# A two-layer encoder step on one core: the query norm behind its projection, zero products at the beginning, joined last outputs, and the final norm in two halves

## The chip, the cores and the metric

The kernel runs on one core of one Trainium2 chip. The metric is device time in microseconds (us), from launch to the end of the program. Three runs of the kernel before gave 2819.73 to 2820.59 us, median 2820.01 us.

## The reference

One step of a hybrid encoder trunk is computed for two request groups that share the weights: 512 new frames and 64 frames of a running stream, 576 tokens together, model width 1024, two layers. Cut to what matters here:

```
x = x + 0.5 * (silu(norm(x) @ w_gate) * (norm(x) @ w_up)) @ w_down        # ffn1, width 2816
h = norm(x); proj = h @ w_in                                              # token mixer
q = rmsnorm(c_q, q_norm) @ w_uq                                           # c_q: 256 columns of proj
y_a = latent attention (8 heads, chunk mask) of q against c_kv            # MLA
y_b = RWKV-7 recurrence (8 heads, 64x64 state), written by chunks of 64
x = x + concat(y_a, y_b) @ w_out
x = x + cross attention(norm(x), 256 memory tokens)
x = x + 0.5 * swiglu(norm(x))                                             # ffn2
y = rmsnorm(x, final_norm)                                                # after both layers
```

All of it is in float32. Every norm is an RMS norm: rsqrt of the mean square over the features, times a gain. The scale of one token is one number, so a norm can be applied before or after a linear projection.

## The kernel before

The activations lie with the features on the 128 partitions and the 576 tokens along the row: x is 8 tiles of 128x576. Where a product needs one accumulator bank, the tokens are cut into two halves `hs` of 288 (HT). A float32 product is done as three products in a rounded format: both operands are split into a high and a low part (`split`, L244 to L249: ScalarE copies the high part, VectorE subtracts to get the low part), and `mm3` (L313 to L317) issues high x high, high x low and low x high into one accumulator. So every weight block of 128x512 costs one ScalarE copy (`whi` or `sh`) and one VectorE subtraction (`wlo` or `sl`) before TensorE can use it.

Feed-forward: the 22 blocks of the inner width go by pairs. The first two pairs (`PLAIN`) are plain products, gate then up (`plain_gate`, `plain_up`); the pairs from 2 to 10 use a scheme of seven products on sums and differences of blocks (`gate`, `up`, `sums`), the sums of the weights being made on VectorE as well (`add` in `factors`). After every second pair `all_outputs` multiplies the finished activations by the output weights `wds` and adds the result to x, one VectorE instruction for each 128x288 block (L521). The last pair, 10, has its outputs alone, with the weights `wd` of its own. The weights come in the order of the list `order`, through a ring of six split blocks (four `whi`/`wlo`, two `sh`/`sl`).

Norm (`Norm`, L360 to L390): ScalarE writes x times the gain as a high part `xnh` (L370), VectorE the low part `xnl` (L371); ScalarE squares (L376), VectorE adds them up in `nacc` (L378), a product with ones sums over the partitions (L386), and `rsqrt` (L300, L349, L350) gives `rstd`, which is applied to the result of the product. So the product starts before the norm is known.

Mixer: the columns of w_in are projected in a list of steps, among them `queries` (two tiles `lx` for c_q, their squares, and the sum of the squares on GpSimd, L851) and, after `rotated`, `normed`: the sum over partitions by a product with ones (L360), `rsqrt` (L300, L349, L350), then c_q times gain and scale (L867) and the split into `qnh`, `qnl`. Attention follows: the value factors `vph`, `vpl`, the keys `kfh`, `kfl` and `kch`, `kcl`, then for each pair of heads the queries `qf` and their split. The products that make them write banks `g`, of which there are two; `sm` is another pair of banks. The recurrence runs beside it: VectorE inverts triangular matrices (L781, L782, tiles `x` of 72 partitions), copies of the state are laid into `VS` (L1036, L1037), and products `pp` (L1052) start the chunks.

The order of the instructions on each engine is made by a scheduler when the program is built, from the order of the code and modelled durations; each engine then runs its list strictly in order, and waits at an instruction whose operand is not there.

The last feed-forward ends in the final norm (`final`, `tail`): squares of x by tile, sums of pairs on VectorE and GpSimd, six products with ones for each half (L1411), `rsqrt`, and the scaled output in six VectorE (L1415) and two GpSimd instructions for each half. The transfers to `y` go out by pairs of tiles.

## Time and profile before

| what | value |
|---|---|
| median of three runs | 2820.01 us |
| the profiled execution: its time | 2819.02 us |
| its span, first to last instruction | 2817.0 us |
| TensorE busy | 2733.7 us (97%) |
| VectorE busy | 2124.5 us (75%) |
| ScalarE busy | 1351.2 us (48%) |
| GpSimd busy | 100.1 us (4%) |
| mean granted TensorE clock | 0.991 |

Engines are PE (TensorE), DVE (VectorE), ACT (ScalarE), POOL (GpSimd) and SP (SyncE, which issues the transfers). The span leaves out 2 us of the execution's own time. A stretch in which TensorE is idle is read from the waits and from windows; what ended an idle stretch stands behind an arrow.

### The profile page before, as it was taken

The numbers are of one execution on the slowest core, as the hardware profiler recorded it, in microseconds if no ns is written. First come the engines' busy times: TensorE is split into PE (matmuls) and PEld (weight loads), VectorE is DVE, ScalarE is ACT, GpSimd is POOL, SyncE is SP. The second block draws the span as 40 slices with busy tenths as digits, with TensorE's granted clock in tenths as the row PEclk, the third lists the DMA queues.
The fourth block names the chain that finished last, engine by engine and source line by source line (L and its number), as shares of the span: only waits on it lengthen the run. The fifth ranks groups of instructions, "written<-read, shape, count | busy, mean of one in ns | idle before, by whom it ended". The sixth has DMA issues, their size and how long they took to land.

```text
span 2817.0 us, 55885 instructions
## 1 busy us (share of the span) xinstructions
PE 2733.7 (97%) x22284; PEld 2629.8 (93%) x22284; DVE 2124.5 (75%) x4356; ACT 1351.2 (48%) x2781; POOL 100.1 (4%) x197
## 2 busy tenths in 40 slices
PE   8999999979999999999999999998999999999998
PEld 8999999968889899999999999997888899999998
DVE  8888876875676678777788777769666765887776
ACT  5544446355544544444444444554555445444443
POOL 0000001010000000000000000012000000000000
PEclk9999999989999999999999999999999999999999
DMA  5333333652233222222223222346433332222221
GB/s 192 101 111 114 112 124 110 158 142 91 92 119 117 72 97 72 92 93 92 94 71 105 91 90 91 109 105 171 118 98 123 98 117 64 91 91 90 92 93 60
DMA packets 187573, 293.21 MB, mean 104 GB/s; under 512 B 87066, under 2 KB 113050, under 8 KB 187138
## 3 DMA queue, kind: packets, MB, share of 16 engines
q1 hardware_dynamic: 185010, 285.46, 32.3%
q0 software_dynamic: 2304, 4.20, 0.6%
q8 instruction: 175, 2.87, 0.4%
q14 instruction: 84, 0.69, 0.1%
HBM read 250.36 MB, written 41.63 MB: 104 GB/s over the span
## 4 chain that ended last, share of the span: by engine, by line
PE 92%; DVE 4%; ACT 2%; issue 1%; DMA 0%; DVEq 0%; SPq 0%; POOL 0%; ACTq 0%
PE b L315 18%; PE b L316 18%; PE b L317 18%; PE mm L315 4%; PE mm L316 4%; PE mm L317 4%; PE g L315 4%; PE g L316 3%; PE g L317 3%; PE sm L1028 2%; PE pp L1028 2%; PE sc L315 2%; PE pp L1052 1%; PE sc L316 1%; PE sc L317 1%; PE tp L981 1%
## 5 line engine op out<-in xcount | busy, mean ns | idle before, releaser
L247 ACT ACTIVATE whi<-wraw 128x512 fp32r<-128x512 f32 (+1 forms) x493 | 305.4, 623 | 543.5 <-PE b L316 264.9
L248 DVE TENSOR_TENSOR wlo<-wraw,whi 128x512 fp32r<-128x512 f32 (+1 forms) x493 | 333.8, 680 | 117.6 <-ACT whi L247 99.9
L317 PE MATMUL b<-s,wlo 128*128 128x288 f32 x1388 | 408.0, 295 | 0.0
L316 PE MATMUL b<-s,whi 128*128 128x288 f32 x1388 | 406.7, 294 | 0.0
L315 PE MATMUL b<-s,whi 128*128 128x288 f32 x1388 | 405.5, 296 | 0.0
L315 PE MATMUL b<-xnh,whi 128*128 128x288 f32 x1168 | 344.5, 298 | 11.5 <-ACT xnh L370 7.6
L316 PE MATMUL b<-xnl,whi 128*128 128x288 f32 x1168 | 346.2, 297 | 3.4 <-DVE xnl L248 1.8
L317 PE MATMUL b<-xnh,wlo 128*128 128x288 f32 x1168 | 343.6, 296 | 0.0
L521 DVE SCALAR_TENSOR_TENSOR x<-b,x 128x288 f32<-128x288 f32 x448 | 196.8, 455 | 132.0 <-PE b L317 131.7
L316 PEld LDWEIGHTS b<-s,whi 128*128 128x128 f32 x1388 | 261.2, 188 | 0.0
L317 PEld LDWEIGHTS b<-s,wlo 128*128 128x128 f32 x1388 | 261.2, 188 | 0.0
L315 PEld LDWEIGHTS b<-s,whi 128*128 128x128 f32 x1388 | 259.5, 188 | 0.0
L315 PEld LDWEIGHTS b<-xnh,whi 128*128 128x128 f32 x1168 | 219.5, 189 | 13.1 <-ACT xnh L370 7.6
L316 PEld LDWEIGHTS b<-xnl,whi 128*128 128x128 f32 x1168 | 220.3, 189 | 5.7 <-DVE xnl L371 2.9
L316 PE MATMUL b<-s,sh 128*128 128x288 f32 x756 | 224.1, 297 | 0.0
L317 PE MATMUL b<-s,sl 128*128 128x288 f32 x756 | 223.1, 296 | 0.0
L315 PE MATMUL b<-s,sh 128*128 128x288 f32 x756 | 223.0, 296 | 0.0
L317 PEld LDWEIGHTS b<-xnh,wlo 128*128 128x128 f32 x1168 | 220.3, 189 | 0.0
L315 PE MATMUL mm<-xnh,whi 128*128 128x288 f32 x688 | 204.2, 298 | 5.2 <-DVE shp L391 1.8
L316 PE MATMUL mm<-xnl,whi 128*128 128x288 f32 x688 | 205.1, 298 | 1.0 <-DVE xnl L371 0.9
L317 PE MATMUL mm<-xnh,wlo 128*128 128x288 f32 x688 | 204.1, 297 | 0.0
L247 ACT ACTIVATE whi<-S 128x512 fp32r<-128x512 f32 x171 | 107.9, 631 | 165.8 <-PE b L316 161.9
(474 smaller groups left out, 7241.4 us busy)
## 6 DMA issues: line engine op xcount, KB each, us to landing
wraw<-in_wgu SPq DMA_DIRECT2D x131, 512.0 KB
wraw<-in_wds SPq DMA_DIRECT2D x48, 512.0 KB
sraw<-in_wgu SPq DMA_DIRECT2D x45, 512.0 KB
wraw<-in_win SPq DMA_DIRECT2D x36, 512.0 KB
wraw<-in_wd SPq DMA_DIRECT2D x21, 512.0 KB
sraw<-in_wds SPq DMA_DIRECT2D x16, 512.0 KB
wraw<-in_wmk SPq DMA_DIRECT2D x16, 512.0 KB
wraw<-in_wmv SPq DMA_DIRECT2D x16, 512.0 KB
```

Source lines behind the costliest of these rows:

```text
L247: ACT.activation(out=h, in_=src, func=AF.Copy)
L248: by.tensor_tensor(out=lo, in0=src, in1=h.bitcast(F32), op=ALU.subtract)
L315: PE.matmul(out, wh, ah, start=first, stop=False, **kw)
L316: PE.matmul(out, wh, al, start=False, stop=False, **kw)
L317: return PE.matmul(out, wl, ah, start=False, stop=last, **kw)
L521: DVE.scalar_tensor_tensor(out=o, in0=p, scalar=0.5, in1=o, op0=ALU.mult, op1=ALU.add)
L981: PE.transpose(pT[0:n, c0:c0 + nq], pe_[e][0:nq, kt * 128:kt * 128 + n], ident[0:nq, 0:nq])
L1028: PE.matmul(o, *f(p4, e), start=(n == 0 and p4 == 0), stop=(n == len(terms) - 1), skip_group_check=True)
L1052: i = PE.matmul(p[:, p4], bk[half(e), p4], ck[half(e), p4, 0:128], start=True, stop=True)
```

## The change

1. Beginning. The transfer of x tile 0 goes ahead of the first weight block and the early constants follow tile 2. If the first weights are given (layer 0, ffn1), 22 products of a zero tile are issued ahead of everything. In every feed-forward the first half (`parts=(0,)`, 24 products) of the first `up` is issued right behind the first gate, ahead of the product with ones of the norm.

2. End of each feed-forward. Pairs 8, 9 and 10 have their outputs together (`last_outputs`): 18 products in one accumulator instead of 12 and 6, and one VectorE addition to x instead of two. The outputs of 8 and 9 no longer stand between the gate and the up of pair 10. The weights come in the new order. In the last feed-forward of the kernel the second group of four tiles is done by halves, and the final norm of half 0 is issued behind the second of the four outputs of half 1.

3. Queries. c_q times gain is split right behind its projection, without the scale of the norm; the sum of the squares moves from GpSimd to VectorE; the scale goes into its own tile `rq` and is multiplied onto `qf` (128x576, once for each of the 8 heads). In the first pair of heads the products take banks `g` and `sm` by turns. The state is loaded into `VS` by two transfers instead of two copies.

4. Final norm. Each half has its own squares, six VectorE additions in a chain, two products with ones instead of six, and the outputs on VectorE and ScalarE alone.

The list of instructions has 14 more on TensorE (22 zero products, less 8 products with ones), 39 fewer on VectorE and 6 more on ScalarE.

```diff
         for k in range(8):
-            if k in (0, 3):
+            if k in (1, 4):
                 given.append(Weights(I["wgu1"][0, 0, len(given)]))
             t = st([128, T], "x")
             SP.dma_start(t, I["x"][k])
             x.append(t)
+            if k == 2:
+                SP.dma_start(cst[:, 0:early], I["cst"][:, 0:early])
...
+        if given:
+
+            z, pz = st([128, 2, HT], "s", F32R), ps1("b")[:, 0:HT]
+            POOL.memset(z[:, 0].bitcast(F32), 0.0)
+            for _ in range(22):
+                PE.matmul(pz, z[:, 0, 0:128], z[:, 0], start=True, stop=True)
...
-            if (p - PLAIN) % 2:
+            if (p - PLAIN) % 2 and p < NF // 2 - 2:
                 order += [[wds[l, (p - PLAIN) // 2, m]] for m in range(4)]
-        order += [[wd[l, PLAIN, g]] for g in range(2)]
+        for g in range(2):
+            order += [[wd[l, PLAIN, g]]] + [[wds[l, (NF // 2 - 2 - PLAIN) // 2, 2 * g + m]] for m in range(2)]
...
+
+            w2 = [take(0 if by_halves else 2) for _ in range(2)]
+            w4 = []
+
+            def some(i, s):
+                p = ps1("b")[:, 0:HT]
+                for f in range(4):
+                    mm3(p, cols(w4[i], f), [t[:, s] for t in acts[f]], f == 0, False)
+                for f in range(2):
+                    end = mm3(p, cols(w2[i // 2], i % 2 * 2 + f), [t[:, s] for t in acts[4 + f]], False, f == 1)
+                o = x[4 * g + i][:, s]
+                DVE.scalar_tensor_tensor(out=o, in0=p, scalar=0.5, in1=o, op0=ALU.mult, op1=ALU.add)
+                return end
+
+            for i in range(4):
+                w4.append(take(0 if by_halves else (2, 2, 2, 1)[i]))
+                for s in hs[0:1] if by_halves else hs:
+                    some(i, s)
+            if by_halves:
+                for i in range(4):
+                    end = some(i, hs[1])
+                    if i == 1:
+                        by_halves(end)
...
         xs, acts = [], []
         for f in range(2 * PLAIN):
-            g = plain_gate()
+            gate_ps = plain(nrm.out)
+
+            up_ps = plain(nrm.out, parts=(0,)) if f == 0 else None
+            g = plain_gate(gate_ps)
...
+
+            acts += up(g, ("rr", "a", "rs") if p == NF // 2 - 3 else None)
             if not end:
                 g = gate()
-            if (p - PLAIN) % 2:
+            if (p - PLAIN) % 2 and p < NF // 2 - 2:
                 all_outputs(acts)
                 acts = []
+        last_outputs(0, acts)
         if final is None:
-            all_outputs(acts)
+            last_outputs(1, acts)
         else:
-            all_outputs(acts, range(4))
             half_done, done = final()
-            outputs(acts, range(4, 8), half_done)
+            last_outputs(1, acts, half_done)
             done()
         ps.close()
         sc.close()
 
     def mixer(l, V, xn):
...
             elif op == "queries":
                 cq = [latent(nrm.rstd()) for j in range(2)]
                 sqs = [squares(t) for t in cq]
-                POOL.tensor_tensor(out=sqs[0], in0=sqs[0], in1=sqs[1], op=ALU.add)
+                DVE.tensor_tensor(out=sqs[0], in0=sqs[0], in1=sqs[1], op=ALU.add)
+
+                qn = []
+                for j in range(2):
+                    h, lo = st([128, T], "qnh", F32R), st([128, T], "qnl", F32R)
+                    ACT.activation(out=h, in_=cq[j], func=AF.Copy, scale=V("qn", j))
+                    DVE.scalar_tensor_tensor(out=lo, in0=cq[j], scalar=V("qn", j), in1=h.bitcast(F32), op0=ALU.mult, op1=ALU.subtract)
+                    qn.append((h, lo))
...
                 ccv = (cch[:, 0], ccl[:, 0])
             elif op == "normed":
-                rq = rsqrt(pv(full(ones, sqs[0:1])), 1.0 / 256, EPS, *rrs(), halves)
-                qn = []
-                for j in range(2):
-                    DVE.scalar_tensor_tensor(out=cq[j], in0=cq[j], scalar=V("qn", j), in1=rq, op0=ALU.mult, op1=ALU.mult)
...
+            turn = [0]
+
+            def bank():
+
+                tags_ = ("g", "g", "sm", "sm") if pr_ == 0 else ("g",)
+                turn[0] += 1
+                return ps1(tags_[(turn[0] - 1) % len(tags_)])
...
-                        p = ps1("g")
+                        p = bank()
                         for k in range(2):
                             queried[0] = mm3(p[:, 0:HT], wp_[1 + 2 * e + k], [t[:, s] for t in qn[k]], k == 0, k == 1)
                         ACT.activation(out=qf[nr, s], in_=p[nr, 0:HT], func=AF.Copy)
                         DVE.tensor_tensor(out=qf[rr, s], in0=p[rr, 0:HT], in1=C("rot")[rr, s], op=ALU.mult)
+                    DVE.tensor_tensor(out=qf, in0=qf, in1=rq, op=ALU.mult)
                     qs.append(split(qf, None, "q"))
...
-                beside(VS, S)
+                for e in range(2):
+                    SP.dma_start(VS[half(e), e], I["state"][l][half(e)])
...
+        def tail(a, prior=None):
             ss, s = ps1("b")[:, 0:HT], hs[a]
-            for k in (1, 3, 4, 6, 5, 7):
-                if k > 3:
-                    ACT.activation(out=qs[k][:, s], in_=x[k][:, s], func=AF.Square)
-                PE.matmul(ss, ones, qs[k][:, s], start=k == 1, stop=k == 7)
+            qs = [st([128, 2, HT], "s")[:, 0] for _ in range(8)]
+            for k in range(8):
+                ACT.activation(out=qs[k], in_=x[k][:, s], func=AF.Square)
+                if 0 < k < 7:
+                    DVE.tensor_tensor(out=qs[k], in0=qs[k - 1], in1=qs[k], op=ALU.add)
+            i = PE.matmul(ss, ones, qs[6], start=True, stop=False)
+            if prior is not None:
+                after(i, prior)
+            PE.matmul(ss, ones, qs[7], start=False, stop=True)
             rsqrt(ss, 1.0 / D, EPS, r[:, s], sq[:, s])
-            for k in (0, 4, 5, 1, 6, 7, 2, 3):
-                if k > 1:
-                    DVE.scalar_tensor_tensor(out=out(k, a), in0=x[k][:, s], scalar=V("fin", k), in1=r[:, s], op0=ALU.mult, op1=ALU.mult)
+            for j in range(4):
+                t = y[2 * j + a]
+                if j < 2:
+                    for i in range(2):
+                        ACT.activation(out=t[:, i], in_=x[2 * j + i][:, s], func=AF.Copy, scale=V("fin", 2 * j + i))
+                    DVE.tensor_tensor(out=t, in0=t, in1=r[:, s].unsqueeze(1).to_broadcast([128, 2, HT]), op=ALU.mult)
                 else:
-                    POOL.tensor_tensor(out=out(k, a), in0=out(k, a), in1=r[:, s], op=ALU.mult)
-                if k % 2:
-                    SP.dma_start(O["y"][k - 1:k + 1, :, s].rearrange("k p t -> p k t"), y[2 * (k // 2) + a])
-        return [lambda a=a: tail(a) for a in range(2)]
+                    for i in range(2):
+                        DVE.scalar_tensor_tensor(out=t[:, i], in0=x[2 * j + i][:, s], scalar=V("fin", 2 * j + i), in1=r[:, s], op0=ALU.mult, op1=ALU.mult)
+                SP.dma_start(O["y"][2 * j:2 * j + 2, :, s].rearrange("k p t -> p k t"), t)
+        return [lambda prior=None, a=a: tail(a, prior) for a in range(2)]
```

On TensorE, at the first norm: the rows before, where `b` are accumulators and L386 is the product with ones.

```order
L316 MATMUL b<-xnl,whi 128x288
L317 MATMUL b<-xnh,wlo 128x288
L316 MATMUL b<-xnl,whi 128x288
L317 MATMUL b<-xnh,wlo 128x288
L386 MATMUL b<-nacc,cst 128x288 x2
L315 MATMUL b<-xnh,whi 128x288
```

The same place in the changed kernel, where that product is L387.

```order
L318 MATMUL b<-xnh,wlo 128x288
L316 MATMUL b<-xnh,whi 128x288
L317 MATMUL b<-xnl,whi 128x288
L318 MATMUL b<-xnh,wlo 128x288
L387 MATMUL b<-nacc,cst 128x288 x2
L316 MATMUL b<-xnh,whi 128x288
```

The product with ones stands behind 72 products instead of 48: the 24 of the first `up` half have come ahead of it.

On VectorE, where the mixer of layer 0 turns to attention: before, L867 applies the norm to c_q (`lx`), the two `qnl` are its low parts and the `vpl` those of the value factors; L781 and L782 belong to the inverse.

```order
L867 SCALAR_TENSOR_TENSOR lx<-lx,narrow,rr 128x576 x2
L782 TENSOR_REDUCE x<-x 72x2x11
L248 TENSOR_TENSOR qnl<-lx,qnh 128x576
L781 TENSOR_TENSOR x<-x 72x2x12x12
L248 TENSOR_TENSOR qnl<-lx,qnh 128x576
L782 TENSOR_REDUCE x<-x 72x2x12
L781 TENSOR_TENSOR x<-x 72x2x13x13
L248 TENSOR_TENSOR vpl<-g,vph 128x512
L782 TENSOR_REDUCE x<-x 72x2x13
L248 TENSOR_TENSOR vpl<-g,vph 128x512
```

In the changed kernel L888 adds the squares, L894 makes the second `qnl`, and L350 and L351 make the scale `rq`.

```order
L888 TENSOR_TENSOR nsq<-nsq 128x576
L894 SCALAR_TENSOR_TENSOR qnl<-lx,narrow,qnh 128x576
...
L350 SCALAR_TENSOR_TENSOR rs<-mm,rs 128x576
L819 TENSOR_REDUCE x<-x 72x2x8
L351 SCALAR_TENSOR_TENSOR rq<-rs,rq 128x576
L818 TENSOR_TENSOR x<-x 72x2x9x9
L819 TENSOR_REDUCE x<-x 72x2x9
L818 TENSOR_TENSOR x<-x 72x2x10x10
L249 TENSOR_TENSOR vpl<-g,vph 128x512
L819 TENSOR_REDUCE x<-x 72x2x10
L249 TENSOR_TENSOR vpl<-g,vph 128x512
```

The two `qnl` have gone ahead of the norm, the two L867 are gone, and between the end of the norm and the first `vpl` stand three instructions of the inverse instead of nine instructions of all kinds.

On VectorE at the end of the program: L521 adds the last outputs to x, L349 and L350 make the scale, L1415 writes outputs.

```order
L521 SCALAR_TENSOR_TENSOR x<-b,x 128x288 x8
L349 SCALAR_TENSOR_TENSOR rs<-b,rs 128x288
L350 SCALAR_TENSOR_TENSOR rstd<-rs,rstd 128x288
L1415 SCALAR_TENSOR_TENSOR s<-x,narrow,rstd 128x288 x6
L349 SCALAR_TENSOR_TENSOR rs<-b,rs 128x288
L350 SCALAR_TENSOR_TENSOR rstd<-rs,rstd 128x288
L1415 SCALAR_TENSOR_TENSOR s<-x,narrow,rstd 128x288 x6
```

In the changed kernel L550 adds the outputs, L1449 adds squares, L1460 and L1463 write outputs.

```order
L550 SCALAR_TENSOR_TENSOR x<-b,x 128x288 x4
L350 SCALAR_TENSOR_TENSOR rs<-b,rs 128x288
L351 SCALAR_TENSOR_TENSOR rstd<-rs,rstd 128x288
L1460 TENSOR_TENSOR s<-s,rstd 128x576 x2
L1463 SCALAR_TENSOR_TENSOR s<-x,narrow,rstd 128x288 x4
L550 SCALAR_TENSOR_TENSOR x<-b,x 128x288
L1449 TENSOR_TENSOR s<-s 128x288 x6
L350 SCALAR_TENSOR_TENSOR rs<-b,rs 128x288
L351 SCALAR_TENSOR_TENSOR rstd<-rs,rstd 128x288
L1460 TENSOR_TENSOR s<-s,rstd 128x576 x2
L1463 SCALAR_TENSOR_TENSOR s<-x,narrow,rstd 128x288 x4
```

The last addition to x now stands behind the whole output of half 0, and the six additions of squares of half 1 behind that.

## Rows read from the trace of the kernel before

**Rows 1.** The page, the shares of the chain of work that ended last.

```profile
...
PE 92%; DVE 4%; ACT 2%; issue 1%; DMA 0%; DVEq 0%; SPq 0%; POOL 0%; ACTq 0%
...
```

**Rows 2.** Waits of TensorE, whole run: us in total, times, longest.

```profile
...
PE g L315 <- DVE vpl L248: 21.3, 2, 10.8
...
PE g L315 <- DVE kfl L248: 5.0, 4, 2.3
PE b L386 <- DVE nacc L378: 4.0, 2, 2.3
...
```

**Rows 3.** Windows: stretch, busy time (count) by engine, then granted clock, DMA.

```profile
...
565.00:570.00 5.00, 0.00 (x0) 0.00 (x0) 5.00 (x10) 2.11 (x4) 2.57 (x2) 0.60 0.43 156
570.00:575.00 5.00, 1.90 (x9) 1.89 (x9) 4.93 (x9) 3.40 (x7) 4.96 (x8) 0.50 0.13 42
575.00:580.00 5.00, 2.70 (x10) 2.03 (x9) 4.52 (x9) 2.83 (x7) 1.68 (x3) 0.50 1.04 262
...
```

**Rows 4.** Timeline of the start, TensorE and VectorE: start, length, idle before.

```profile
...
12.20 0.44 PE L317 MATMUL b<-xnh,wlo 128*128 128x288 f32 x1
12.44 0.73 PE L315 MATMUL b<-xnh,whi 128*128 128x288 f32 x2
...
18.40 0.29 PE L316 MATMUL b<-xnl,whi 128*128 128x288 f32 x1
18.53 0.29 PE L317 MATMUL b<-xnh,wlo 128*128 128x288 f32 x1
21.11 1.24 PE L386 MATMUL b<-nacc,cst 128*128 128x288 f32 x4 [2.29 <-DVE nacc L378]
...
20.31 0.75 DVE L378 TENSOR_TENSOR nacc<-nacc,nsq 128x576 f32<-128x576 f32 x1
```

**Rows 5.** Timeline, all engines, where the first mixer turns to attention.

```profile
...
559.92 1.41 POOL L851 TENSOR_TENSOR nsq<-nsq 128x576 f32<-128x576 f32 x1 [15.80 <-ACT nsq L684]
...
561.38 1.24 PE L360 MATMUL mm<-nsq,cst 128*128 128x288 f32 x4 [0.80 <-POOL nsq L851]
...
566.27 0.74 DVE L350 SCALAR_TENSOR_TENSOR rr<-rs,rr 128x576 f32<-128x576 f32 x1
...
573.10 0.55 PE L315 MATMUL g<-whi,cch 128*128 128x256 f32 x1 [10.48 <-DVE vpl L248]
...
573.29 0.68 DVE L248 TENSOR_TENSOR vpl<-g,vph 128x512 fp32r<-128x512 f32 x1
...
```

**Rows 6.** Waits of TensorE, 390 to 422 us, first feed-forward end.

```profile
...
PE g L386 <- DVE nacc L378: 1.4, 1, 1.4
PE mm L316 <- DVE xnl L371: 0.9, 1, 0.9
PE b L316 <- DVE xnl L248: 0.7, 1, 0.7
PE b L315 <- ACT xnh L247: 0.6, 1, 0.6
PE mm L315 <- DVE x L521: 0.3, 1, 0.3
```

**Rows 7.** The page, costliest groups: busy us, mean ns, idle before.

```profile
...
L247 ACT ACTIVATE whi<-wraw 128x512 fp32r<-128x512 f32 (+1 forms) x493 | 305.4, 623 | 543.5 <-PE b L316 264.9
L248 DVE TENSOR_TENSOR wlo<-wraw,whi 128x512 fp32r<-128x512 f32 (+1 forms) x493 | 333.8, 680 | 117.6 <-ACT whi L247 99.9
...
L521 DVE SCALAR_TENSOR_TENSOR x<-b,x 128x288 f32<-128x288 f32 x448 | 196.8, 455 | 132.0 <-PE b L317 131.7
...
```

**Rows 8.** Windows in the attention of layer 0, same columns.

```profile
...
600.00:650.00 50.00, 49.05 (x572) 42.49 (x568) 32.96 (x91) 28.38 (x79) 2.88 (x7) 1.00 0.31 94
...
```

**Rows 9.** Timeline of the last stretch, TensorE and VectorE.

```profile
...
2803.00 3.07 PE L1411 MATMUL b<-s,cst 128*128 128x288 f32 x12
...
2805.00 3.74 DVE L1415 SCALAR_TENSOR_TENSOR s<-x,narrow,rstd 128x288 f32<-128x288 f32 x6
...
2809.64 3.73 DVE L1415 SCALAR_TENSOR_TENSOR s<-x,narrow,rstd 128x288 f32<-128x288 f32 x6
...
```

More of the change, by code (lines that the diff above doesn't have):

```diff
@@ L200, in C @@
         return cst[:, o:o + (n or m)]
-    NW = 640
+    NW = 600
     narrow = st([128, NW], "narrow")
@@ L528, in all_outputs, with last_outputs, plain @@
                 outputs(acts, range(m, m + per))
-        def plain(act):
-            ps = [ps1("b")[:, 0:HT] for _ in hs]
-            for i in range(2):
+        def last_outputs(g, acts, by_halves=None):
+            w2 = [take(0 if by_halves else 2) for _ in range(2)]
[18 more added lines that the diff above has]
+                        by_halves(end)
+        def plain(act, ps=None, parts=(0, 1)):
+            ps = ps or [ps1("b")[:, 0:HT] for _ in hs]
+            for i in parts:
                 w = take(2)
@@ L537, in plain, with plain_gate @@
                         mm3(p, cols(w, k), [t[:, s] for t in act[4 * i + k]], i + k == 0, i * k == 3)
-            return list(zip(hs, ps))
-        def plain_gate():
+            return ps
+        def plain_gate(ps):
             gs = []
-            for s, p in plain(nrm.out):
+            for s, p in zip(hs, ps):
                 g = tmp()
@@ L547, in plain_gate, with plain_up @@
             return gs
-        def plain_up(gs, tag):
+        def plain_up(ps, gs, tag):
             act = [st([128, T], tag or turn("rr", "a", "rs"), F32R) for _ in range(2)]
-            for (s, p), g in zip(plain(nrm.out), gs):
+            for s, p, g in zip(hs, ps, gs):
                 u = tmp()
@@ L595, in gate, with up @@
             return g
-        def up(g):
-            acts = [(st([128, T], "xnh", F32R), st([128, T], "xnl", F32R)) for f in range(2)]
+        def up(g, tags=None):
+            acts = [tuple(st([128, T], t or turn(*tags), F32R) for t in (("xnh", "xnl") if tags is None else (None, None))) for f in range(2)]
             for f, e, t in sums(xs, lambda f, e: tmp()):
@@ L1391, in final @@
         r, sq = st([128, T], "rstd"), st([128, T], "rs")
-        y, qs = ([st([128, 2, HT], "s") for _ in range(8)] for _ in range(2))
-        qs = [t.rearrange("p a b -> p (a b)") for t in qs]
-        for k in range(4):
-            ACT.activation(out=qs[k], in_=x[k], func=AF.Square)
-            if k % 2:
-                (DVE if k == 1 else POOL).tensor_tensor(out=qs[k], in0=qs[k - 1], in1=qs[k], op=ALU.add)
-        def out(k, a):
-            return y[2 * (k // 2) + a][:, k % 2]
-        for k in range(2):
-            for a in range(2):
-                ACT.activation(out=out(k, a), in_=x[k][:, hs[a]], func=AF.Copy, scale=V("fin", k))
```

17 lines of the change are left out of this document (7 added, 10 removed).

## Prediction

> **What bounds the kernel now.** I read the chain first: TensorE holds 92% of it, VectorE 4%, ScalarE 2% [rows 1]. At full clock the products run back to back, so only what leaves TensorE idle, or slow, can be gained, and some 8% is open. The waits of TensorE come next [rows 2]: the longest by far is where each mixer turns to attention, 21.3 us in two pieces. The windows there [rows 3] show VectorE full and TensorE without any work for five microseconds, and a granted clock of 0.60 and then 0.50, half speed. Then the start, by its timeline [rows 4], the ends of the feed-forwards, by the waits in their stretch [rows 6], and the tail, by its timeline [rows 9]. The sum is made against the profiled execution, 2819.02 us, 1 us under the median of 2820.01; the span is 2817.0.
>
> **Beginning.** TensorE ends the gate at about 18.7 and waits 2.29 us for the last `nacc` [rows 4]. In the changed order 24 products of `up` stand ahead of the product with ones. One product starts 0.13 us after the other at 18.40 and 18.53 [rows 4], so they are 24 x 0.13 = 3.2 us of work, which covers the 2.29; the product with ones then comes at 21.9 instead of 21.11, with the second half of `up` next. Gain 2.3. Tile 0 of x and the first weights change places, one transfer issue; I take 0.5 us off the first product for it. The 22 zero products run while nothing else can. The products up to 12.44 start 0.24 us apart and those at 18.40 0.13 [rows 4], so the clock stood at half in the first 5 us. About 20 products lie there, 20 x 0.11 = 2.2 us if they were bound by the clock, nothing if by their operands; the row before it is VectorE's, so I take nothing and keep 2.2 for the range. Beginning: 2.8 (0 to 5).
>
> By the Trainium skill, "TensorE: Matmul & The Clock Gate", section "What's actually happening", the throttled state is the default and activity releases it. The trace agrees, 0.24 and then 0.13 between products. By that rule the zero products would hand on a clock that is up, and the sum would be 2.2 us lower; by the operand wait it stays.
>
> **The turn to attention, twice.** In layer 0 the order before is: GpSimd adds the squares (1.41 from 559.92), TensorE sums them at 561.38, ScalarE and VectorE make the scale by 567.0, and then VectorE and ScalarE apply it, split the queries, and split the value factors by 573.97; TensorE waits 10.48 us to 573.10 [rows 5]. In the changed order the queries are split before, and nothing but three pieces of the inverse stands between the scale and the first `vpl`. Nine instructions become three; of the 573.29 - 567.0 = 6.3 us between the scale and the second `vpl`, two applications and two low parts at 0.75 each (3.0) are gone. Against that, the addition now stands in VectorE's queue, behind the inverse, and I put its end 1.9 us later, while the pieces of the inverse (the rest of VectorE's five full microseconds, [rows 3]) come 4 to 5 us later than before. The products of the value factors also wait for the scale when they take an `sm` bank, since that bank holds its sum. So the gap doesn't close, it shrinks: 2 to 3 us of it, and I take 2.5 a layer, 5 for both. The bounds are 0, if the inverse that is pushed back becomes the last to arrive, and the 6.3 us of the chain, 12.6 for both.
>
> The multiplication by `rq`, 8 a layer and 16 in all, is a 128x576 operation like L350, 0.74 us [rows 5]: 12 us of VectorE. In the attention VectorE is busy for 32.96 of 50 us and TensorE for 49.05 [rows 8], so they lie beside products; I take nothing, with 12 as the price where that cover is gone.
>
> **Ends of the feed-forwards.** At the first end the waits sum to 3.9 us: 1.4 for `nacc`, 0.9 for the next norm's `xnl`, 0.7 and 0.6 for the low and high part of the last pair's activations, 0.3 for x [rows 6]. The same five stand at the two other ends that lead into a norm, where they are 4.5 each by the same view; at the last one only the pair of 0.7 and 0.6 can stand, and is half of it. That makes 3.9 + 4.5 + 4.5 + 0.7 = 13.6. After: the joined outputs begin with pairs 8 and 9, which were done long before; 36 products (4.8 us) stand ahead of the first that needs pair 10, so the 0.6 and 0.7 go. VectorE loses 16 additions of 0.455 at each end [rows 7], 7.3 us out of about 30 in a stretch where it held TensorE up, and the last x are 18 products (2.4 us) apart, not 6, so that the norm's parts of one tile are done when the next comes. What is late next is the last tile's own chain (addition, square, `nacc`); the product it must meet is still some 35 further on, so I leave 0.2 at each of three ends. Gain 13 (5 to 15). What the new order asks is five product sets in a row without outputs between; the splits keep 0.62 + 0.68 us each [rows 7], and VectorE has fewer additions there than before.
>
> **Final norm.** Of the 24 passes with ones 12 come behind the last output product, 3.07 us [rows 9], and 12 before; now 4 and 4. One pass is 3.07 / 12 = 0.256 us; ahead of the end of the last product 12 - 4 = 8 of them go, 2.0 us. Behind it the order is worse: the last addition to x stands behind the whole output of half 0 on VectorE, and six dependent additions of squares behind that. From the last product's end I count 3.5 us to the end of that addition (half 0's scale and outputs, 4.3 us, begin about 1 us before that product ends, since their last ScalarE step needs a tile that the product reads), then six additions at 0.455 like L521's [rows 7], 2.7; four passes with ones, 1.0, and 0.2 to hand on; three ScalarE steps taken at 0.5, 1.5; the scale in two pieces and the outputs in two of 128x576 and four of 128x288, 0.9 + 1.5 + 1.9 = 4.3; and from the last output to the end 2817.0 - 2813.4 = 3.6 as before [rows 9]. That is 16.8; before it was 2817.0 - 2803.1 = 13.9 [rows 9]. So 2.9 lost and 2.0 gained, 1 us slower (from 3 slower to 2 faster).
>
> **Sum.** 2.8 + 5 + 13 - 1 = 19.8; 2819.02 - 19.8 = 2799.2, and I say 2799.
>
> **Rivals.** A: the turn to attention does not shrink. VectorE is full there [rows 3], and every piece of the inverse taken out of the way of the queries comes back behind them, while the recurrence's first products wait for the inverse. The gain there is then nothing, or 4.5 us a layer is lost: 2804 to 2813, middle 2808. For it speaks the full VectorE; against it that the products of keys and queries (waits for `kfl`, 5.0 us in four, [rows 2]) depend on `vpl`'s place and not on the inverse.
>
> B: at the ends of the feed-forwards only the wait for the last pair's parts goes, 1.3 at each of three ends and 0.7 at the last, 4.6; the norm's own chain is as long as before, and its waits of 1.4 and 0.9 stay. 2799.2 + 8.4 = 2807.6. Against it: the additions that go are on the engine that ended these waits.
>
> C: TensorE gets enough work in the turn that its clock stays up. Products that ran at 0.50 fill 1.90 of the five microseconds from 570 and 2.70 of the next [rows 3], 4.6 us that would be 2.3, and as much behind them, some 5 us a layer: 2789. Against it: half of the idle stretch remains.
>
> The Trainium skill, in the same page under "Why this matters for your kernels", warns against idle stretches between bursts, since one brings the clock back to half. The trace agrees, 0.60 and 0.50 with TensorE empty. By that rule a gap that only shrinks still costs the half clock, which speaks for the sum and against C.
>
> D, the slower one: the splits of the joined weights come late. Six blocks fill the whole ring, so each block of the second group can be split only when its place is released by the first, and the split stands in VectorE's queue behind additions that themselves wait for TensorE. One split is 0.62 + 0.68 = 1.3 us [rows 7]; 12 blocks at 4 ends, if each came late by all of it, are 62 us, by half of it 31. With the 13 us of the ends gone: 2799.2 + 13 + 31 = 2843. It decides for slower from about 0.3 us for each of the 48, since the other parts gain 6.8. Against it: the shortest distance from release to use that I find in the order is 18 products, 2.4 us.
>
> **How the numbers follow.** The forecast has 0.62, its own range being 2792 to 2806; A 0.14, B 0.08, C 0.10, D 0.06. The range 2789 to 2811 leaves out D, half of C and the far part of A and of the forecast, about 0.17. A measurement of this kernel tells 0.2%, 5.6 us, from no change, so faster is below 2814.4: the forecast, C, B and nearly all of A, less what mishaps of size may add, 0.88. Within: 0.06, from the upper ends of A and B with a worse tail. Slower: 0.06, D.
>
> **What would show it.** Start: no wait at the first product with ones, and the first product near 7.1. Turn: the wait for `vpl` 7 to 9 us instead of 10.5 and 10.8, half clock still there, and the first key products 2 to 3 us earlier against the end of the projection. Ends: the five waits below 0.5 us together. Tail: about 17 us from the last output product to the end of the span. It would be wrong if a new wait of TensorE stood in the last outputs for a split, or if the inverse became the releaser of the recurrence's products with a longer wait than before.

## The result and the profile after

The changed kernel takes 2796.16 us (median of 5 runs, 2792.61 to 2798.45), the kernel before 2820.01 (5 runs, 2819.15 to 2821.78): ratio 0.9913, 95% interval 0.9899 to 0.9926. That is 23.9 us faster; the forecast was 2799, the range 2789 to 2811. The profiled executions have spans of 2817.0 and 2794.4. The sum came out near, but by luck and not by its terms: the beginning was taken three times too small, the gain in the turn to attention was lost again behind it, and only the ends were right.

I read the waits of TensorE first, over the whole run (us in total, times, longest).

```profile
...
PE b L1450 <- DVE s L1449: 6.6, 1, 6.6
PE g L316 <- DVE kfl L249: 6.5, 3, 3.1
PE sm L316 <- DVE rs L350: 6.1, 2, 3.1
PE pp L1076 <- DMA DI<-d: 4.5, 2, 3.1
...
PE g L316 <- DVE vpl L249: 1.2, 2, 0.8
...
```

Beside [rows 2]: the wait for `vpl` has gone from 21.3 to 1.2, and in its place stand three others in the same stretch, 6.1 for the scale `rs`, 6.5 for `kfl` and 4.5 for the inverse that comes back as `DI`. Before, no product waited for `DI`, so one of the two signs that the prediction named for being wrong has come. The longest single wait is now in the last microseconds, 6.6.

To see where the time went I took, in both traces, the moment of the same product at the borders of the stages (us of the span; the last column is what the stage gained). The first projection of a mixer is its first product of `kk`; the last output product is taken to end 0.13 us behind its start, where the next one could start.

| border, the same product in both | before | after | earlier by | gained in the stage |
|---|---|---|---|---|
| 144th product of the first feed-forward | 34.8 | 28.7 | 6.1 | 6.1 |
| first projection of mixer 0 behind its norm | 434.8 | 423.0 | 11.8 | 5.7 |
| second feed-forward, layer 0 | 1012.7 | 997.4 | 15.3 | 3.5 |
| first projection of mixer 1 behind its norm | 1829.1 | 1803.9 | 25.2 | 9.9 |
| second feed-forward, layer 1 | 2406.7 | 2383.4 | 23.3 | -1.9 |
| end of the last output product | 2803.0 | 2776.2 | 26.8 | 3.5 |
| end of the span | 2817.0 | 2794.4 | 22.6 | -4.2 |

The beginning of the changed kernel, TensorE's timeline (start, length, idle before):

```profile
...
1.12 5.65 PE L412 MATMUL b<-s 128*128 128x288 f32 x22 [1.12 <-POOL s L410]
6.57 0.44 PE L316 MATMUL b<-xnh,whi 128*128 128x288 f32 x1
6.81 0.44 PE L317 MATMUL b<-xnl,whi 128*128 128x288 f32 x1
...
7.27 0.30 PE L317 MATMUL b<-xnl,whi 128*128 128x288 f32 x1
7.40 0.43 PE L318 MATMUL b<-xnh,wlo 128*128 128x288 f32 x2
...
21.45 1.13 PE L387 MATMUL b<-nacc,cst 128*128 128x288 f32 x4
...
```

The first product stands at 6.57 instead of 7.56, and the product with ones at 21.45, without an idle stretch ahead of it, where [rows 4] had 2.29. The products stand 0.24 us apart at first and 0.13 from 7.27 on, where [rows 4] had 0.24 until 12.44, so the clock left its half about 5 us sooner.

The trace corrects a count made ahead of the prediction: 96 products run ahead of the product with ones at this first norm, not 72. The scheduler has put the whole first `up` there, 48 products, and not its first half of 24 alone; in both second feed-forwards it is 72. VectorE shows it too: it reads the accumulators of `up` (L586) right behind those of the gate (L577),

```profile
...
25.63 0.81 DVE L577 TENSOR_TENSOR t<-b,rstd 128x288 f32<-128x288 f32 x2
26.36 0.81 DVE L586 TENSOR_TENSOR t<-b,rstd 128x288 f32<-128x288 f32 x2
...
```

and in the kernel before 3.5 us behind (L544 at 25.39, L553 here):

```profile
...
28.90 0.46 DVE L553 TENSOR_TENSOR t<-b,rstd 128x288 f32<-128x288 f32 x1
...
```

With 48 products the 6.1 us follow: 48 x 0.133 = 6.4 us of work no longer stand behind the norm, and the first product behind it starts 0.24 us later (22.21 against 21.97).

The windows of 5 us of the changed kernel show what the wait alone does not: stretch, busy time (count) of PE, PEld, DVE, ACT, POOL, then granted clock, DMA share, GB/s. The column of the clock starts at 1.00 in both, though the distances between the products show half clock there; and a product that lies in two windows is counted in both.

```profile
...
5.00:10.00 5.00, 4.33 (x23) 3.86 (x22) 4.33 (x7) 4.71 (x9) 0.00 (x0) 1.00 1.02 388
10.00:15.00 5.00, 4.76 (x34) 4.43 (x35) 5.00 (x8) 5.00 (x9) 0.00 (x0) 1.00 1.04 414
15.00:20.00 5.00, 5.00 (x40) 5.00 (x40) 4.85 (x8) 2.61 (x5) 0.00 (x0) 1.00 1.15 484
...
```

The same windows of the kernel before:

```profile
...
5.00:10.00 5.00, 2.42 (x8) 2.07 (x9) 3.24 (x5) 4.31 (x8) 0.00 (x0) 1.00 1.01 349
10.00:15.00 5.00, 4.23 (x19) 3.62 (x18) 5.00 (x9) 5.00 (x9) 0.00 (x0) 1.00 1.04 411
15.00:20.00 5.00, 3.44 (x22) 2.98 (x22) 5.00 (x8) 3.95 (x7) 0.00 (x0) 1.00 1.19 493
...
```

The two windows from 10 to 20 us count 74 products where they counted 41: the added products fill the waits between the tiles of x, not only the one behind the last tile.

The end of the first feed-forward of the changed kernel, in a window of 27 us, same columns:

```profile
...
385.00:412.00 27.00, 27.00 (x203) 26.79 (x202) 16.33 (x26) 11.95 (x19) 0.00 (x0) 1.00 0.34 115
...
```

TensorE is busy for 27.00 of 27.00, and no wait is left of the five of [rows 6]; the two other ends that lead into a norm show none either. (Before, the second had the same five and the third four, with 1.8 for `shp` in place of the norm's own.) VectorE is busy for 16.33 of the 27.

The turn of the first mixer in the changed kernel, timeline of all engines, answers to [rows 5]:

```profile
...
549.49 0.75 DVE L888 TENSOR_TENSOR nsq<-nsq 128x576 f32<-128x576 f32 x1
...
550.28 1.24 PE L361 MATMUL mm<-nsq,cst 128*128 128x288 f32 x4 [0.80 <-DVE nsq L888]
...
553.76 0.76 DVE L350 SCALAR_TENSOR_TENSOR rs<-mm,rs 128x576 f32<-128x576 f32 x1
...
554.58 0.58 PE L316 MATMUL sm<-whi,cch 128*128 128x256 f32 x1 [3.06 <-DVE rs L350]
...
558.42 0.40 ACT L248 ACTIVATE kfh<-g 64x288 fp32r<-64x288 f32 x1
...
561.51 0.44 DVE L249 TENSOR_TENSOR kfl<-g,kfh 64x288 fp32r<-64x288 f32 x1
...
563.82 0.46 DVE L249 TENSOR_TENSOR kfl<-g,kfh 64x288 fp32r<-64x288 f32 x1
...
564.42 0.58 PE L316 MATMUL g<-qnh,whi 128*128 128x288 f32 x1 [3.11 <-DVE kfl L249]
...
578.46 0.33 PE L1076 MATMUL pp<-DI,A 64*64 64x64 f32 x2
...
581.11 0.67 PE L1076 MATMUL pp<-DI,A 64*64 64x64 f32 x14 [1.32 <-DMA DI<-d]
...
```

And its window while the clock is at half, which answers to [rows 3]:

```profile
...
553.40:577.30 23.90, 19.20 (x77) 17.35 (x77) 20.64 (x43) 11.47 (x25) 2.12 (x4) 0.50 0.64 161
...
```

TensorE waits 3.06 for the scale, since the `sm` bank holds its sum; then 3.11 for the bank that a `kfl` frees (the one at 563.82). The first `kfl` could run at 558.8, when its high part `kfh` was done; it stands on VectorE behind four pieces of the inverse and a weight split until 561.51, and the others behind it. At last the recurrence issues its first product with `DI` and waits 1.32 for the rest of it (3.1 in layer 1). The clock is at half for all of 23.9 us, where before it was for 17.1 and 3.4; in layer 1 it is at half for 20.4 in three pieces, as long as before.

How much earlier the same products come than before, counted from the first projection of each mixer (us), tells what became of this:

| product | layer 0 | layer 1 |
|---|---|---|
| first key product (`g<-ckvh,whi`) | 6.3 | 7.2 |
| first product with `DI` | 3.9 | 5.3 |
| first output product of the attention (`yah`) | 4.5 | -3.1 |
| second feed-forward | 3.5 | -1.9 |

So the turn did get shorter, by more than the 2 to 3 us of the prediction, part of it was lost again up to the recurrence, and in layer 1 all of it, and more, in the rest of the attention.

The tail of the changed kernel, timeline of TensorE and VectorE, answers to [rows 9]:

```profile
...
2776.02 0.29 PE L318 MATMUL b<-xnh,wlo 128*128 128x288 f32 x1
2776.14 1.43 DVE L1460 TENSOR_TENSOR s<-s,rstd 128x576 f32<-128x576 f32 x2
...
2777.49 1.80 DVE L1463 SCALAR_TENSOR_TENSOR s<-x,narrow,rstd 128x288 f32<-128x288 f32 x4
2779.20 0.46 DVE L550 SCALAR_TENSOR_TENSOR x<-b,x 128x288 f32<-128x288 f32 x1
2779.57 3.26 DVE L1449 TENSOR_TENSOR s<-s 128x288 f32<-128x288 f32 x6
...
2782.89 1.33 PE L1450 MATMUL b<-s,cst 128*128 128x288 f32 x2 [6.58 <-DVE s L1449]
...
```

The last output product starts at 2776.02; the last addition to x at 2779.20, behind the outputs of half 0 (L1460, L1463), and the product with ones waits 6.58 for the sums (L1449) behind that.

### The profile page after: what moved, and what is told of

Its sections match the earlier page's. It is cut to its first block, busy times and chain, and to the rows that moved or that the text cites. A ratio compares the mean times of both kernels' runs of the same rounds, so it can differ in the third digit from the quotient of the medians.

```text
span 2794.4 us, 55844 instructions
## 1 busy us (share of the span) xinstructions
PE 2740.6 (98%) x22290; PEld 2639.7 (94%) x22290; DVE 2102.2 (75%) x4317; ACT 1352.5 (48%) x2787; POOL 86.3 (3%) x189
## 4 chain that ended last, share of the span: by engine, by line
PE 94%; DVE 3%; ACT 2%; DMA 1%; issue 0%; SPq 0%; DVEq 0%; ACTq 0%
PE b L318 19%; PE b L316 19%; PE b L317 18%; PE mm L316 4%; PE mm L318 4%; PE mm L317 4%; PE g L316 3%; PE g L317 3%; PE g L318 3%; PE sm L1076 2%; PE sc L316 2%; PE pp L1076 1%; PE pp L1100 1%; PE sc L317 1%; PE sc L318 1%; PE tp L1029 1%
## 5 line engine op out<-in xcount | busy, mean ns | idle before, releaser
L317 PE MATMUL b<-s,whi 128*128 128x288 f32 x1376 | 403.0, 294 | 0.0
L316 PE MATMUL b<-s,whi 128*128 128x288 f32 x1376 | 399.4, 295 | 0.0
L316 PE MATMUL b<-xnh,whi 128*128 128x288 f32 x1128 | 332.4, 296 | 1.5 <-ACT whi L248 1.5
L317 PE MATMUL b<-xnl,whi 128*128 128x288 f32 x1128 | 332.2, 295 | 0.7 <-DVE xnl L372 0.7
L318 PE MATMUL b<-xnh,wlo 128*128 128x288 f32 x1128 | 331.3, 295 | 0.0
L316 PEld LDWEIGHTS b<-xnh,whi 128*128 128x128 f32 x1128 | 211.9, 188 | 2.5 <-ACT whi L248 2.2
L317 PEld LDWEIGHTS b<-xnl,whi 128*128 128x128 f32 x1128 | 212.3, 188 | 1.3 <-DVE xnl L372 1.1
L318 PEld LDWEIGHTS b<-xnh,wlo 128*128 128x128 f32 x1128 | 211.7, 188 | 0.0
L529 DVE SCALAR_TENSOR_TENSOR x<-b,x 128x288 f32<-128x288 f32 x320 | 140.2, 457 | 84.7 <-PE b L318 84.6
```

The lines of the kernel that those rows point to most:

```text
L316: PE.matmul(out, wh, ah, start=first, stop=False, **kw)
L317: PE.matmul(out, wh, al, start=False, stop=False, **kw)
L318: return PE.matmul(out, wl, ah, start=False, stop=last, **kw)
L529: DVE.scalar_tensor_tensor(out=o, in0=p, scalar=0.5, in1=o, op0=ALU.mult, op1=ALU.add)
```

## The experiments

Each run was taken beside runs of the kernel before, whose median lay between 2819.15 and 2820.10 us; the ratios are against these. Differences between two medians of different runs carry that spread of 1 us.

**Which part is worth what: the query part undone.** The third part as in the kernel before, all else changed.

```diff
+                POOL.tensor_tensor(out=sqs[0], in0=sqs[0], in1=sqs[1], op=ALU.add)
+                rq = rsqrt(pv(full(ones, sqs[0:1])), 1.0 / 256, EPS, *rrs(), halves)
...
-                    DVE.tensor_tensor(out=qf, in0=qf, in1=rq, op=ALU.mult)
-                        p = bank()
+                        p = ps1("g")
```

> The changed kernel with its third part undone (queries applied and split behind the norm, sum of squares on GpSimd, no rq, banks g alone, state by copies); beginning, ends and final norm stay changed. Theory from the two traces: the 10.5 us wait for vpl was replaced by waits of 3.1 for the scale, 3.1 for kfl and 1.3 to 3.1 for the inverse, at half clock, so the part is worth 1.7 us for both layers: 2798. By the prediction's term it is worth 5: 2801. By rival A it costs time: 2790 to 2796. In every case the wait for vpl of about 10.5 us comes back.

Measured: 2796.22 us (2795.79 to 2796.81), ratio 0.9916 (0.9903 to 0.9930). The wait came back as expected, by this kernel's waits of TensorE from 535 to 600 us,

```profile
...
PE g L316 <- DVE vpl L249: 10.5, 1, 10.5
PE g L316 <- DVE kfl L249: 2.4, 1, 2.4
...
```

and the time did not move: the part is worth nothing here, less than my theory of 1.7 and than the prediction's 5, and A's loss isn't seen either. By the borders this nothing is a sum: against this run the changed kernel is 1.9 us faster in the mixer of layer 0 and 1.9 slower in that of layer 1.

**The joined outputs undone** in the three feed-forwards that lead into another stage.

```diff
-            if (p - PLAIN) % 2 and p < NF // 2 - 2:
+            if (p - PLAIN) % 2 and (final is None or p < NF // 2 - 2):
                 all_outputs(acts)
...
+        if final is None:
+            all_outputs(acts)
```

> The changed kernel with the outputs of pairs 8, 9 and 10 apart again in the three feed-forwards that lead into another stage; the last feed-forward stays joined. Theory: the three ends are worth 15.6 us by the two traces, 2812. By the prediction's term 12.4: 2808.5. By rival B, where only the wait for the last pair's parts goes, about 4: 2800. The waits of 0.6 and 0.7 for xnh and xnl and of 1.4 to 1.8 for nacc come back.

Measured: 2809.56 us (2808.74 to 2811.54), ratio 0.9965 (0.9952 to 0.9977): the joining is worth 13.4 us. The waits at the first end are back, by its view from 385 to 420 us,

```profile
...
PE mm L316 <- DVE x L529: 3.1, 1, 3.1
PE b L317 <- DVE xnl L249: 0.7, 1, 0.7
PE b L316 <- ACT xnh L248: 0.6, 1, 0.6
```

with the one for the norm in another place (3.1 for x instead of 1.4 for `nacc`). It stands between the two sizes that were written down, nearer to the prediction's 12.4, and far from rival B's 4. By the borders the first end is worth 6.1 and the two others 8.7; the rest of the difference, 1.4 the other way, lies in the start and the mixers, outside the edit.

**Without the zero products.**

```diff
-            for _ in range(22):
-                PE.matmul(pz, z[:, 0, 0:128], z[:, 0], start=True, stop=True)
```

> The changed kernel without the 22 zero products. Theory: the clock is worth it, since the first products start 0.13 us apart and not 0.24 once it is up at 7.2 us: 2.5 us slower, 2798.7. Rival (the prediction's choice): the operands pace the first products, no difference, 2796.

Measured: 2797.43 us (2794.91 to 2799.22), ratio 0.9919 (0.9906 to 0.9933). By the trace the clock rises at 9.9 us instead of 7.2 and the 144th product is at 29.0 instead of 28.7. So the zero products are worth 0.3 us at the start; the 1.3 between the medians lies within the spread of either. The operands pace the first products.

**The final norm as before**, with the joined outputs.

```diff
-            i = PE.matmul(ss, ones, qs[6], start=True, stop=False)
+            for k in (1, 3, 4, 6, 5, 7):
+                PE.matmul(ss, ones, qs[k][:, s], start=k == 1, stop=k == 7)
```

> The changed kernel with the final norm as before (six products with ones for each half, GpSimd for two outputs), outputs still joined and by halves. Theory: behind the last output product it needs 13.9 us instead of 18.2, and 2.0 more of products with ones ahead: 2 us faster, 2794. By the prediction's term (1 slower for the new norm) 2795. Rival: the new norm is a gain by itself, 2798 to 2800.

Measured: 2793.67 us (2791.22 to 2795.42), ratio 0.9906 (0.9893 to 0.9920), 2.5 us faster than with the new norm. Its last product ends at 2776.1 and its span at 2789.0, 13 us instead of 18.2, and 2.0 more lie ahead in products with ones: by the borders the new norm costs 3.3. The runs of the two overlap, so it is the trace that shows that the new norm by itself costs time, and the medians agree.

**The first up half behind the gate again**, in all four feed-forwards.

```diff
-            up_ps = plain(nrm.out, parts=(0,)) if f == 0 else None
+            up_ps = None
```

> The changed kernel with the first up half behind the gate's evacuation again, in all four feed-forwards. Theory: only the wait of about 2.3 us for nacc at the first norm comes back, and up to 1 us at each of the three others where the norm arrives late: 2798.5 to 2801. Rival: the lighter VectorE already covers the later three and the zero products bring the first norm forward, so 1 us or less: 2797.

Measured: 2807.32 us (2803.95 to 2813.65), ratio 0.9954 (0.9940 to 0.9968): 11 us slower, far beyond both. At the start its windows show why, with the columns as above:

```profile
...
10.00:15.00 5.00, 3.26 (x17) 2.56 (x18) 5.00 (x9) 5.00 (x10) 0.00 (x0) 0.97 1.04 413
15.00:20.00 5.00, 4.21 (x19) 3.63 (x19) 4.90 (x8) 3.02 (x6) 0.00 (x0) 0.69 1.09 457
...
```

The windows count 36 products in ten microseconds instead of 74, and the clock falls (0.69) behind a window in which TensorE was busy for 3.26 of 5 us. The 144th product is at 33.5, 4.8 us later than in the changed kernel. The rest lies elsewhere: the ends give 3.6 us less, and 11.1 us are lost in the mixer of layer 0, whose code is the same, but whose attention the scheduler has put in another order (294 products between the last chunk's first product with `DI` and the first with `yah`, 256 in the changed kernel), while layer 1, which has the order of 256 here, gains 2.3. The profiled execution is the slowest of the five, 2813.65, so these sum to more than the 11 of the medians.

**Another order in the final norm.**

```diff
+                sums_(0, q0, range(8))
+                sums_(1, q1, range(4))
                 for i in range(4):
                     end = some(i, hs[1])
-                    if i == 1:
-                        by_halves(end)
+                    if i < 3:
+                        sums_(1, q1, [4 + i])
+                    if i == 1:
+                        prior = end
+                    if i == 3:
+                        tail_(0, q0, prior)
+                tail_(1, q1)
```

> The changed kernel with another order in the final norm: the squares and their sums of half 1 are made as each tile of x is done, and the scale and outputs of half 0 stand behind the last addition to x on VectorE, not ahead of it. Theory: the last addition starts right behind the last product instead of 3.1 us later, and the six dependent sums of 3.3 us are done by then; 13 us instead of 18.2 from the last product to the end: 5 us faster, 2791. Rival: the outputs of half 0 (4.3 us) only move into the way of those of half 1, 2 us or less: 2794.

Measured: 2790.31 us (2788.52 to 2792.10), ratio 0.9897 (0.9884 to 0.9911), 5.9 us faster than the changed kernel by the medians, 4.8 by the borders of the last two stages. From its timeline:

```profile
...
2774.74 0.46 DVE L1456 TENSOR_TENSOR s<-s 128x288 f32<-128x288 f32 x1 [0.51 <-ACT s L1454]
...
2776.17 0.46 DVE L550 SCALAR_TENSOR_TENSOR x<-b,x 128x288 f32<-128x288 f32 x1 [0.97 <-PE b L318]
...
2778.15 0.44 ACT L301 ACTIVATE rs<-rstd 128x288 f32<-128x288 f32 x1
2778.49 0.43 ACT L1454 ACTIVATE s<-x 128x288 f32<-128x288 f32 x1
...
2778.97 0.75 PE L1464 MATMUL b<-s,cst 128*128 128x288 f32 x2 [1.39 <-ACT s L1454]
...
2780.95 1.80 DVE L1474 SCALAR_TENSOR_TENSOR s<-x,narrow,rstd 128x288 f32<-128x288 f32 x4
...
2782.67 0.45 DVE L350 SCALAR_TENSOR_TENSOR rs<-b,rs 128x288 f32<-128x288 f32 x1
...
```

The last addition starts at 2776.17 right behind its product, and the last sum (L1456) at 2774.74, ahead of it. From the last product to the end there are 14.3 us, more than the 13 I wrote. The last square of half 1 (L1454) could start at 2776.63, when its x is done, but stands on ScalarE behind the three steps of half 0's scale until 2778.49, and the product with ones waits 1.39 for it; then the scale of half 1 (L350 at 2782.67) stands on VectorE behind half 0's outputs.

**Without the multiplication by rq.** The attention's queries are left without the scale of their norm.

```diff
-                    DVE.tensor_tensor(out=qf, in0=qf, in1=rq, op=ALU.mult)
```

> The changed kernel without the multiplication of the queries by the scale rq, so the attention's queries are left without their norm: 16 operations of 0.74 us on VectorE less. Theory: in the attention it costs time behind the chunks, where layer 1 lost what its turn had gained; 3 to 6 us faster, 2790 to 2793. Rival (the prediction's choice): it lies beside products, no difference, 2796.

Measured: 2801.14 us (2796.51 to 2802.41), ratio 0.9932 (0.9920 to 0.9945): 5 us slower with 12 us of VectorE taken away. Both expectations miss. By the borders it loses in layer 1, which gets 5.3 us slower than in the kernel before, and its two attentions have yet another order (285 products counted as above). The multiplication's own cost is nothing that this shows; what the scheduler makes of any edit in this stage is worth several microseconds.

**Banks g alone.**

```diff
-                tags_ = ("g", "g", "sm", "sm") if pr_ == 0 else ("g",)
+                tags_ = ("g",)
```

> The changed kernel with banks g alone in the first pair of heads. Theory: the products of the value factors then wait for the first vpl instead of for the scale that frees the sm bank, 1 to 2 us later, and the first key products with them; the inverse ends the stretch anyway: within 1 us, 2796. Rival: the sm banks are what shortens the turn, 3 to 5 us slower, 2800.

Measured: 2791.57 us (2791.55 to 2798.43; three of four runs at 2791.6), ratio 0.9908 (0.9894 to 0.9921). The waits of TensorE in its first turn:

```profile
...
PE g L316 <- DVE vpl L249: 5.8, 1, 5.8
PE g L316 <- DVE kfl L249: 3.2, 2, 2.7
...
```

TensorE waits 5.8 for `vpl` and 3.2 for `kfl`; no product waits for `DI`. By the borders each mixer gains 3.4 us against the kernel before in this execution, and keeps what the turn gained: the first product with `DI` comes 3.4 us earlier too, in both layers, and the rest of the attention has the order of 256 in both. The turn by `sm` banks doesn't help, and may cost some microseconds; the runs of the two overlap.

**The query part alone**, on banks g, in the kernel before.

```diff
-                POOL.tensor_tensor(out=sqs[0], in0=sqs[0], in1=sqs[1], op=ALU.add)
+                DVE.tensor_tensor(out=sqs[0], in0=sqs[0], in1=sqs[1], op=ALU.add)
...
+                    DVE.tensor_tensor(out=qf, in0=qf, in1=rq, op=ALU.mult)
```

> The kernel before with the query part alone, on banks g alone (split behind the projection, sum on VectorE, rq applied to qf, state by transfers). Theory: the wait of 10.5 us for vpl goes to 3 to 5, the recurrence starts 2 to 3 us earlier in each layer: 2814 to 2816. By the prediction's term 2815. Rival: VectorE is full in the turn, nothing is gained: 2820.

Measured: 2820.11 us (11 runs, 2818.47 to 2824.94), ratio 1.0004 (0.9995 to 1.0013): no difference, against my theory. In the profiled execution the wait for `vpl` in layer 0 is 5.8 and the mixers gain 2.7 and 3.1 us, but 2.1 are lost ahead of the first mixer, where the clock is at half for 3.4 us from 21.3, and 2.9 between the mixers, in code that was not touched. Ahead of the first mixer TensorE, VectorE, ScalarE and GpSimd have the same lists of instructions as in the kernel before. So in this execution the part does gain 5.8 in its own stages, and why the other stages are slower here stays open.

**The beginning alone**, in the kernel before.

```diff
+            for _ in range(22):
+                PE.matmul(pz, z[:, 0, 0:128], z[:, 0], start=True, stop=True)
...
+            up_ps = plain(nrm.out, parts=(0,)) if f == 0 else None
```

> The kernel before with the beginning part alone: order of the first transfers, zero products, and the first up half ahead of the product with ones in all feed-forwards. Theory: the 24 products fill the waits between the tiles of x as well as the one for nacc: 6.1 us at the start and up to 1 at the later norms, 2813 to 2814. By the prediction's term 2.8: 2817.

Measured: 2811.32 us (2810.15 to 2812.35), ratio 0.9969 (0.9958 to 0.9981): 8.2 us. By the borders 6.2 are at the start, 1.2 between the mixers, and 1.3 in the first mixer, whose instructions are the same in the same order.

**Two versions made from these.** The early sums with the queries of the kernel before:

```diff
+                    if i < 3:
+                        sums_(1, q1, [4 + i])
...
-                    DVE.tensor_tensor(out=qf, in0=qf, in1=rq, op=ALU.mult)
```

> The order of the final norm from the run with the early sums, together with the queries as in the kernel before. Theory: the query part with mixed banks was worth nothing, so as fast as the early sums alone: 2790. By the prediction's term for the queries 2795. Rival: the two query forms differ by what the scheduler makes of the rest, 2786 to 2794.

Measured: 2791.23 us (2790.59 to 2791.51), ratio 0.9898 (0.9884 to 0.9911), as the early sums alone. And the early sums with the new queries on banks g:

```diff
+                    if i < 3:
+                        sums_(1, q1, [4 + i])
...
+                tags_ = ("g",)
```

> The early sums of the final norm together with the new queries on banks g alone. Theory: with the sm banks the first products of the recurrence are issued ahead of the inverse and wait for it, with the g banks they are not; the query part is then worth about 4.6 us: 2786. Rival: the run with g banks was only a lucky execution: 2790 as without.

Measured: 2788.84 us (2786.16 to 2789.76), ratio 0.9886 (0.9871 to 0.9901). It is the fastest here, and beats both kernels: 7.3 us under the changed one. Against the version with the old queries it is 2.4 us, and the runs of the two, taken side by side, don't overlap: the query part on banks g is worth about half of the 4.6 that I expected. Its trace has layer 1's mixer 0.2 us slower than before where the run with banks g alone had it 3.4 faster, with the same instructions in the same order.

## Why the prediction was right, and where its steps were not

**Beginning: mis-sized.** The step that failed is "24 x 0.13 = 3.2 us of work, which covers the 2.29". In the built order 48 products stand ahead of the product with ones, not 24, and they do not stand behind the gate: they stand among its products, each tile of x that lands feeds more of them, and they fill the waits between the tiles too. 48 x 0.133 = 6.4, less 0.24, is the 6.1 of the start; of these 4.8 go when `up` stands behind the gate again. Alone the part is worth 8.2 us, 6.2 of them at the start. The first product came 1.0 us earlier, not 0.5. The zero products were taken at nothing, and the run without them shows 0.3. "TensorE: Matmul & The Clock Gate" of the Trainium skill, "What's actually happening", says that activity releases the clock; the trace agrees, 7.2 against 9.9 us, but the products that this would speed up wait for operands.

**The turn to attention: right there, lost behind it.** The wait for `vpl` shrank more than forecast, to 1.2 for both layers, and though three waits took its place the first product with `DI` came 3.9 and 5.3 us earlier, where the text had taken 2.5 a layer. The step that failed is that this gain reaches the end of the mixer, with the multiplication "beside products" and the rest of the attention as before: 3.5 us are left in layer 0, and layer 1 loses 1.9. The part as built is worth nothing undone (2796.22 against 2796.16), and on banks g nothing alone (2820.11 against 2819.52), but 2.4 with the early sums.

Two things are shown on the way. The waits moved along VectorE's queue: the text had named the `sm` bank that holds the sum of the scale, and the inverse (rival A, whose mechanism this is, though not with its loss); it had not seen that the first query products need the bank that a `kfl` frees, and that these stand in the same queue behind the inverse. And the loss of layer 1 lies behind the first product with `DI`, where its attention has another order: with 294 products between the last chunk's first product with `DI` and the first with `yah`, that stretch from the first product with `DI` took 222.5 to 228.6 us (five attentions), with 241 or 256 of them 214.4 to 221.1 (with the 285 of the run without `rq`, 218.6 and 223.7). That the order is the cause is not shown, since no run changed it alone; but the three runs of the new queries on banks g, which never have the order of 294, keep their gain in five of six mixers (2.7 to 3.4 us).

**Ends: right.** 13 forecast, 12.4 of it for the three that were undone, where 13.4 were measured, and the waits are gone as said; even the 0.2 left at each end isn't there. By the borders of that run they are worth somewhat more, 14.8. Rival D, late splits, does not occur: TensorE is busy for all 27 us of the window that holds the first joined outputs.

**Final norm: right in sign, too small.** Forecast 1 us slower, measured 2.5, by the borders 3.3. Of the 16.8 us counted behind the last product 18.2 were there; 3.5 to the end of the last addition is what the trace has, but the six sums take 3.26 and not 2.7, each waiting for the one before, and the products with ones run at half clock.

**The sum.** 2.8 + 5 + 13 - 1 against 8.2 + 0 + 13.4 - 2.5 = 19.1: two errors of five microseconds each way cancelled, which is luck. The 4.8 us that are left to 23.9 are in no part that was undone by itself. The borders of the traces have them: start 6.1 and 1.2 at the later norms, mixers 1.6 (which the run with the old queries has as well), the three ends 14.4, the last joined outputs 2.6 by the run with the old norm, the new norm -3.3, together the 22.6 by which the spans differ. The medians move by 2 us or so.

## What to carry to other kernels

Work moved ahead of a wait is worth more than that wait where the operands arrive one by one: count the idle time in the whole stretch that it can fill, not the last piece, and count the moved instructions in the order that was built. Where an engine is full, a chain taken out of its queue uncovers the next consumer of the same queue; follow the queue to the second and third product before pricing the first, and follow the gain to the end of the stage: an order made anew can take it back. In an engine's own order, an output that nobody waits for must not stand ahead of the last input that everybody waits for.

## What was not expected of the hardware

The granted clock fell again in stretches of 3.4 us away from the turn: at 795.7 and 2184.9 in the changed kernel, where TensorE had been busy for 3.20 and 2.49 of the 4 us ahead, and at 21.3 in the run with the queries alone, where it had been busy for 1.72, with the wait of 2.3 us for `nacc` among them. The kernel before has the same list of instructions there, the same wait and 1.71 of 4 us busy, and its clock stayed up. The same instructions gained 3.4 us in a mixer in one execution and lost 0.2 in another, with 20.5 and 23.9 us at half clock. For edits of this size one profiled execution does not rank two orders of this stage.
